# Token preparation by rows: most token tiles modulated and split token-major, then turned by transposing transfers

## Chip, cores and metric

The kernel runs on one core of one Trainium2 chip. The metric is the device time of one launch in microseconds (us), the median of the runs shown. Engines are named as the profile names them: PE is TensorE (its weight loads are PEld), DVE is VectorE, ACT is ScalarE, POOL is GpSimd, SP is SyncE, which here only issues transfers.

## What is computed

Two layers over 2048 latent and 256 context tokens of width 1024. Each layer is an RMS norm with a modulation (a scale and a shift per feature, one pair for the latent stream and one for the context), an input projection, four token mixers with SiLU gates (Fourier, attention, convolution, pooling), and an output projection:

```
h  = rmsnorm(x,  norm_g) * (1.0 + scale)   + shift       # latent, 2048 x 1024
hc = rmsnorm(xc, norm_g) * (1.0 + scale_c) + shift_c     # context, 256 x 1024
parts = split(h @ w_in)                                  # q, k, v, Fourier u, gates, conv, pool inputs
out   = concat([o_f, o_att, o_c, o_p]) @ w_out
x_new = x + gate * out                                   # and the same for xc in layer 0
```

The change is in how the kernel builds `h` and `hc` in the form that the input projection wants.

## The kernel before, in words

The tokens lie in five blocks: b0 is the 256 context tokens, b1 to b4 are 512 latent tokens each. A block is prepared in tiles of 128 tokens, four to a latent block and two to the context, 36 over both layers. `prep(L, b)` turns a block into tiles `h{b}{part}{i}`: features on the partitions, tokens along the row, as a pair of 16-bit numbers (part 0 the rounded value, part 1 the remainder), since the products on PE are made of three 16-bit passes.

For one tile of 128 tokens `prep` loads it (L251), squares and sums it on ACT (L261), makes the reciprocal root on POOL (L240, L241), scales the tile by it on ACT (L263), turns it on PE by eight 128x128 transposes into PSUM (L271), applies scale and shift on DVE, which reads that PSUM (L275, eight instructions, one for each 128 features), rounds to 16 bits on ACT (L278) and takes the remainder on POOL (L279). It is a generator and yields once for each tile, so that its caller can lay the tiles between other work.

The token stage of a layer is `token_groups`. Its `block(b)` makes the products that are wanted token by token: two `fourier_in` (48 matmuls of 256 columns each, L342), `keys` and `values` (96 of 128 columns each, L332), and two `queries` (L342 again). `keys` and `queries` go on through norm and rotary positions: POOL does L240, L241, L407 (the rotary table times the gain), L438, L451 and L461, and DVE does L420, L431, L436 and L440. Their results are stored by SP: `kd` (L452), `qd` (L462), and the Fourier input `ud` (L376). Each yield of `block(b)` runs one step of the preparation of a later block: in layer 0 of the next one, in layer 1 of the one two places on, in the order b1, b2, b3, b4, b0. Layer 1 prepares b1 and b2 beside the end of layer 0's output projection (L1166). PE then goes from the last queries of one block straight to the first `fourier_in` of the next, which reads all features of the tokens it covers.

A scheduler decides the final order of the instructions; each engine then runs its own list in that order and waits by semaphores. Tiles come from pools with a fixed number of buffers; a tile is reused when its last reader is done. `dg` (L1120, L1125) is an existing helper of the output projection: a diagonal matrix is multiplied by a matrix of ones on PE, so that a row of 512 numbers stands on all partitions.

Of the kernel before, what the change touches and what calls it, by code (L numbers as in the profile page):

```python
# [10 lines left out]
F32 = mybir.dt.float32  # L11
F32R = mybir.dt.float32r
F16 = mybir.dt.float16
BF16 = mybir.dt.bfloat16
ACTF = mybir.ActivationFunctionType
ALU = mybir.AluOpType
# [4 lines left out]
D = 1024  # L21
KC = 8
# [4 lines left out]
BLK = [(0, 256)] + [(256 + 512 * i, 512) for i in range(4)]  # L27
# [15 lines left out]
def hybrid_kernel(ctx: ExitStack, tc: tile.TileContext, T, out):  # L43
    nc = tc.nc
    PE, ACT, DVE, POOL, SP = nc.tensor, nc.scalar, nc.vector, nc.gpsimd, nc.sync
# [18 lines left out]
    sm = pool("sm", 3)  # L64
# [16 lines left out]
    def big(shape, dt, name):  # L81
        return slot.tile(shape, dt, tag="s", name=name)
# [13 lines left out]
    id32 = const.tile([128, 128], F32, name="id32")  # L96
# [10 lines left out]
    ones = const.tile([128, 128], F32, name="ones")  # L107
# [96 lines left out]
    aff = {}  # L204
# [23 lines left out]
    def alloc_h(b):  # L228
        n = BLK[b][1]
        per = 2048 // n  # L230
        hT[b] = [[big([128, per, n], F16, f"h{b}{part}{i}") for i in range(KC // per)] for part in range(2)]

    def h_ap(b, part, k, t0, n, nk=1):
        per = 2048 // BLK[b][1]
        t = hT[b][part][k // per]
        return t[:, k % per, t0:t0 + n] if nk == 1 else t[:, k % per:k % per + nk, t0:t0 + n]

    def rms_scale(ss, n, count, tag):
        ms = sm.tile([128, 8], F32, tag=tag, name=tag)[:, 0:n]
        POOL.tensor_scalar(out=ms, in0=ss, scalar1=1.0 / count, scalar2=EPS, op0=ALU.mult, op1=ALU.add)  # L240
        POOL.tensor_tensor(out=ms, in0=ms, in1=nh[:, 0:n], op=ALU.pow)  # L241
        return ms

    def prep(L, b, tp, psum):

        s = 1 if b == 0 else 0
        g0, n = BLK[b]

        def load(t):
            xt = tp.tile([128, D], F32, tag="x", name="xt")  # L250
            (SP if L == 0 and b < 2 else ACT).dma_start(out=xt, in_=source(L, g0 + t * 128))  # L251
            return xt

        ahead = load(0)
        for t in range(n // 128):
            xt = ahead
            if (t + 1) * 128 < n:
                ahead = load(t + 1)
            xn = tp.tile([128, D], F32, tag="xn", name="xn")
            ss = sm.tile([128, 1], F32, tag="ss", name="ss")  # L260
            ACT.activation(out=xn, in_=xt, func=ACTF.Square, accum_out=ss)  # L261
            rstd = rms_scale(ss, 1, D, "rx")
            ACT.activation(out=xn, in_=xt, func=ACTF.Copy, scale=rstd)  # L263
            yield
            if t == 0:
                alloc_h(b)
            for half in range(2):
                pt = psum()
                for j in range(4):
                    k = 4 * half + j  # L270
                    PE.transpose(out=pt[:, j * 128:(j + 1) * 128], in_=xn[:, k * 128:(k + 1) * 128], identity=id32)  # L271
                h32 = tp.tile([128, 4, 128], F32, tag="h32", name="h32")
                for j in range(4):
                    k = 4 * half + j
                    DVE.tensor_scalar(out=h32[:, j, :], in0=pt[:, j * 128:(j + 1) * 128], scalar1=aff[L][0][:, 0, k, s:s + 1],  # L275
                                      scalar2=aff[L][0][:, 1, k, s:s + 1], op0=ALU.mult, op1=ALU.add)
                hi = h_ap(b, 0, 4 * half, t * 128, 128, 4)
                ACT.copy(out=hi, in_=h32)  # L278
                POOL.tensor_tensor(out=h_ap(b, 1, 4 * half, t * 128, 128, 4), in0=h32, in1=hi, op=ALU.subtract)  # L279
# [849 lines left out]
    def source(L, tok):  # L1129

        if L > 0:
            return xd[tok:tok + 128]
        return T["ctx"][tok:tok + 128] if tok < NCTX else T["x"][tok - NCTX:tok - NCTX + 128]
# [51 lines left out]
    TOKEN = {"s": 4, "ko": 1, "qo": 1, "rope": 1, "gq": 1}  # L1185

    gate_w = {}
    with ExitStack() as st:
        tp = TagPool(st, tc, "s0", {**TOKEN, "x": 4, "xn": 2, "h32": 2, "row": 1})
        ws = []  # L1190
        ahead = prep(0, 0, tp, aux_bank)
        for c in range(4):
            for i, _ in enumerate(modulate(0, c, aux_bank, tp, True)):
                if (c, i) == (0, 3):
                    steps(ahead, 1)
                if (c, i) == (2, 3):
                    ws += [load_w(0, *TOKEN_W[0])]
        SP.dma_start(out=gain, in_=T["gains"].partition_broadcast(128))
        ws += [load_w(0, *TOKEN_W[1])]
        SP.dma_start(out=edge, in_=T["k_edge"])  # L1200
        SP.dma_start(out=invw, in_=T["k_invw"])
        SP.dma_start(out=cd, in_=T["k_cd"])
        affine(0)
        for w in ws:
            unscale(0, w[1])
        steps(ahead, 9)
        block = token_groups(0, tp, ws)
        for b in range(5):
            ahead = prep(0, b + 1, tp, aux_bank) if b + 1 < 5 else iter(())
            if b == 4:  # L1210
                gate_w[0] = load_w(0, *GATE_W[0:2], True)
            for _ in block(b):
                steps(ahead, 1)
            steps(ahead, 9)
# [27 lines left out]
    for L in range(DEPTH):  # L1242
# [19 lines left out]
        right = ExitStack()  # L1262
# [19 lines left out]
        with ExitStack() as st:  # L1282
            pp = TagPool(st, tc, f"p{L}", {"mix": 1, "ml": 2, "gate": 1, "x": 2})
            late = project(L, blocks[-2:], lambda shape, dt, name: pp.tile(shape, dt, "mix" if name == "dg" else name, name), 2)
            steps(late, 1)
            steps(fill, 1 << 30)
            if L + 1 < DEPTH:
                w_mode(f"t{L + 1}", True)
                with ExitStack() as st2:
                    sp = TagPool(st2, tc, f"s{L + 1}", {**TOKEN, "s": 2, "x": 2, "xn": 1, "h32": 2}, "right")  # L1290
                    with tc.issue_after(load_mark[0]):
                        block = token_groups(L + 1, sp, [])
                    for b in blocks[0:2]:
                        for _ in prep(L + 1, b, sp, mx_bank):
                            steps(late, 3)
                    for i, b in enumerate(blocks):
                        ahead = prep(L + 1, blocks[i + 2], sp, mx_bank) if i + 2 < 5 else iter(())
                        if i == 3:
                            gate_w[L + 1] = load_w(L + 1, *GATE_W[0:2], True)
                        for _ in block(b):  # L1300
                            steps(ahead, 1)
                            steps(late, 8)
                        steps(ahead, 9)
                        if i == 0:
                            steps(late, 1 << 30)
            steps(late, 1 << 30)
# [98 lines left out]
```

## Time and profile before

| what | value |
|---|---|
| time, median of 3 runs | 2219.25 us (2217.25 to 2222.85) |
| the profiled execution's own time | 2221.17 us |
| its span, first to last instruction | 2219.4 us |
| granted clock of PE, mean | 0.990 |
| busy, share of the span | PE 96%, DVE 64%, ACT 55%, POOL 42% |
| layer 0's token stage, blocks b1 to b4 | 67.7 to 205.2 us |
| layer 1's token stage with the end of the projection | about 1094 to 1330 us |

The profile is one execution. Its page gives the busy time of each engine and a strip of 40 slices of the span; its views give groups of instructions by line, a timeline, and sums over windows. A granted clock of 1.00 is the full speed of PE (2.4 GHz), 0.50 the lower level (1.2 GHz). "What ended an idle time" is the instruction whose semaphore came last.

### The profile page before, as it was taken

What the parts mean: (1) busy time and instruction counts of PE and PEld (TensorE: products, weight loads), DVE (VectorE), ACT (ScalarE), POOL (GpSimd) and SP (SyncE); (2) the same over time, 40 slices, a digit from 0 to 9 for tenths busy, and PEclk for the clock granted to TensorE, in tenths of its full rate; (3) what the DMA queues carried; (4) which work ended last, traced back from release to release, by engine and by line L of the source; (5) the groups of instructions that cost most, each with busy time, mean ns of one, the idle gap of its engine ahead of it and who ended that gap; (6) DMA issues with size and microseconds to landing.
All of it is one profiled execution on the core that took longest, in us unless ns stands there. A gap on an engine that the chain in (4) does not pass through costs nothing. (4 is left out here: it accounts for less than half of the span.)

```text
span 2219.4 us, 41113 instructions
## 1 busy us (share of the span) xinstructions
PE 2136.6 (96%) x16207; PEld 1287.1 (58%) x16207; DVE 1411.0 (64%) x2661; ACT 1216.8 (55%) x2265; POOL 931.7 (42%) x998
## 2 busy tenths in 40 slices
PE   7999989989999999999899999999999999989999
PEld 3998545655556555555456995555455555555544
DVE  3654777456687878676575554522678787877533
ACT  4653445346677767555554534334477676766600
POOL 2786543214455556233233862001356355543300
PEclk9999989999999999999999999999999999999999
DMA  8433554551212122222454333335221221223133
GB/s 324 141 101 96 178 165 160 203 155 48 65 46 69 58 71 79 95 71 69 171 200 134 118 100 114 110 105 169 71 65 33 68 63 46 72 88 99 42 102 123
DMA packets 182639, 237.95 MB, mean 107 GB/s; under 512 B 47178, under 2 KB 132526, under 8 KB 182446
## 3 DMA queue, kind: packets, MB, share of 16 engines
q1 hardware_dynamic: 159854, 205.96, 28.4%
q10 hardware_dynamic: 22592, 29.37, 4.2%
q8 instruction: 127, 2.08, 0.4%
q14 instruction: 66, 0.54, 0.1%
HBM read 161.48 MB, written 69.34 MB: 104 GB/s over the span
## 5 line engine op out<-in xcount | busy, mean ns | idle before, releaser
L319 PE MATMUL fl<-h,w 128*128 128x512 f16 (+1 forms) x2592 | 595.5, 368 | 0.4 <-ACT z L504 0.2
L1007 POOL TENSOR_TENSOR pl<-p,ph 128x512 f16<-128x512 f32 (+1 forms) x292 | 355.2, 1216 | 517.9 <-ACT p L1006 435.0
L319 PEld LDWEIGHTS <-w 128*128 128x128 f16 x3456 | 331.2, 99 | 362.0 <-issue 38.8
L1005 ACT ACTIVATE ph<-st 128x512 f16<-128x512 f32 (+1 forms) x584 | 348.7, 597 | 239.2 <-PE st L1001 213.3
L959 DVE TENSOR_REDUCE mp<-mx 128x1 f32<-128x512 f32 (+1 forms) x648 | 394.7, 627 | 114.4 <-PE mx L958 111.7
L1166 PE MATMUL fl<-wo,ml 128*128 128x512 f16 x1632 | 378.9, 380 | 1.4 <-ACT gate L1126 1.1
L1006 ACT ACTIVATE p<-st 128x512 f32<-128x512 f32 (+1 forms) x584 | 349.0, 598 | 25.2 <-DVE pl L1007 23.7
L1007 DVE TENSOR_TENSOR pl<-p,ph 128x512 f16<-128x512 f32 (+1 forms) x292 | 233.1, 798 | 83.5 <-ACT p L1006 67.9
L1166 PEld LDWEIGHTS <-ml 128*128 128x128 f16 x1632 | 158.9, 98 | 184.2 <-issue 6.4
L995 PEld LDWEIGHTS <-ph 128*128 128x128 f16 x2320 | 169.6, 98 | 124.3 <-ACT ph L1005 26.8
L995 PE MATMUL pv<-V,ph 128*128 128x130 f16 x2320 | 222.7, 220 | 11.3 <-ACT ph L1005 10.9
L958 PE MATMUL mx<-kst,qhh 128*128 128x512 f16 x512 | 188.1, 379 | 15.2 <-DVE mp L959 12.2
L319 PE MATMUL st<-h,w 128*128 128x512 f16 (+1 forms) x864 | 195.4, 376 | 3.6 <-DVE r L436 3.6
L1000 PE MATMUL st<-qhh,kst 128*128 128x512 f16 x512 | 193.9, 379 | 2.5 <-ACT p L1006 2.3
L1001 PE MATMUL st<-qlm,k 65*128 65x512 f16 x512 | 195.1, 381 | 0.0
L993 PE MATMUL pv<-V,pl 128*128 128x66 f16 x2320 | 169.1, 193 | 4.1 <-DVE pl L1007 2.1
L342 PEld LDWEIGHTS <-h 128*128 128x128 f16 x1632 | 159.9, 98 | 20.6 <-POOL h L279 0.7
L993 PEld LDWEIGHTS <-pl 128*128 128x128 f16 x2320 | 132.6, 97 | 44.0 <-POOL pl L1007 6.0
L1171 DVE TENSOR_TENSOR fl<-fl,gate 128x512 f32<-128x512 f32 x68 | 47.4, 697 | 99.8 <-PE fl L1166 99.7
L145 POOL TENSOR_TENSOR root<-root,ph__105 128x2 f32<-128x2 f32 (+1 forms) x28 | 20.3, 726 | 207.6 <-DVE root L144 197.7
L157 ACT ACTIVATE ml<-mix,f 128x1024 f16<-128x1024 f32 x34 | 39.1, 1151 | 113.6 <-PE fl L1166 80.3
L332 PEld LDWEIGHTS <-h 128*128 128x128 f16 x1728 | 98.5, 98 | 0.7
(300 smaller groups left out, 3024.4 us busy)
## 6 DMA issues: line engine op xcount, KB each, us to landing
wm<-in_w_mod_dram SPq DMA_DIRECT2D x48, 512.0 KB, 4.5
wst<-in_w_in_dram SPq DMA_DIRECT2D x44, 512.0 KB, 4.2
mix<-mixd SPq DMA_DIRECT2D x34, 512.0 KB, 4.4
zd<-z SPq DMA_DIRECT2D x64, 256.0 KB, 2.2
wst<-in_w_out_dram SPq DMA_DIRECT2D x32, 512.0 KB, 4.5
xd<-x SPq DMA_DIRECT2D x18, 512.0 KB, 3.0
xt<-xd ACTq DMA_DIRECT2D x18, 512.0 KB, 4.4
x<-in_x_dram SPq DMA_DIRECT2D x16, 512.0 KB, 5.2
```

The lines of the kernel that those rows point to most:

```text
L319: last = PE.matmul(out=ps, lhsT=w[:, wp, k, :], rhs=h_ap(b, hp, k, 0, n), start=(k == 0 and i == 0), stop=(k == KC - 1 and i == 2))
L342: PE.matmul(out=ps[:, t], lhsT=h_ap(b, hp, k, (2 * i + t) * 128, 128), rhs=w[:, :, wp, k, :], start=(k == 0 and j == 0), stop=(k == KC - 1 ...
L958: mark[0] = PE.matmul(out=ps, lhsT=qhh[:, t * 128:(t + 1) * 128], rhs=kk, start=True, stop=True).ins
L959: DVE.tensor_reduce(out=mp[:, t, i:i + 1], in_=ps, axis=AX.X, op=ALU.max)
L993: PE.matmul(out=pv[t // 2][:, t % 2, 0:66], lhsT=p, rhs=v[:, 0:66], start=False, stop=(kt == nk - 1), skip_group_check=True)
L995: PE.matmul(out=pv[t // 2][:, t % 2, :], lhsT=p, rhs=v, start=(kt == 0 and t % 2 == 0), stop=False, skip_group_check=True)
L1000: mark[0] = PE.matmul(out=ps, lhsT=self.k_tile(0, kt), rhs=qhh, start=True, stop=False).ins
L1001: PE.matmul(out=ps, lhsT=self.k_tile(1, kt)[0:65, :], rhs=qlm[0:65, :], start=False, stop=True)
L1005: ACT.activation(out=ph, in_=ps, func=ACTF.Exp, scale=1.0 / LOGIT)
L1006: ACT.activation(out=p32, in_=ps, func=ACTF.Exp, scale=1.0 / LOGIT)
L1007: (POOL if kt % 2 == 0 else DVE).tensor_tensor(out=pl, in0=p32, in1=ph, op=ALU.subtract)
L1166: PE.matmul(out=ps, lhsT=ml[:, mp, k, :], rhs=wo[k][:, wp, half * 512:(half + 1) * 512], start=(k == 0 and j == 0), stop=(k == KC - 1 and ...
```

## The change

For layer 1, and for b2, b3 and b4 of layer 0, `prep` hands over to a new function, `prep_rows`; the two tiles of b0 and the four of b1 in layer 0 stay as they were. That is 30 of the 36 tiles. A tile stays token-major through norm, modulation and split; DVE multiplies it by the reciprocal root and the scale row (L290) and adds the shift row (L291); ACT rounds it (L292); POOL takes the remainder (L293); and SP turns the two halves by transposing transfers from SBUF to SBUF (L276). A latent tile needs four of these, a context tile two, 116 in all. They are issued when the next tile has been worked on. The scale and shift rows are made once for each layer and stream (three times) by `affine_rows`: two diagonal tiles on DVE (L250), four matmuls with ones (L255), four copies on ACT.

```
-            (SP if L == 0 and b < 2 else ACT).dma_start(out=xt, in_=source(L, g0 + t * 128))
+            SP.dma_start(out=xt, in_=source(L, g0 + t * 128))      # in prep, now only layer 0, b0 and b1
+        if L or b > 1:
+            yield from prep_rows(L, b, tp, psum)
+            return
...
+    def affine_rows(L, s, psum):
+        for a in range(2):
+            dg = big([128, 8, 128], F32, "dg")
+            DVE.tensor_tensor(out=dg, in0=id32.unsqueeze(1).to_broadcast([128, 8, 128]),
+                              in1=aff[L][0][:, a, :, s].unsqueeze(2).to_broadcast([128, 8, 128]), op=ALU.mult)
+            r = big([128, 1024], F32, f"row{a}")
+            for half in range(2):
+                pg = psum()
+                PE.matmul(out=pg, lhsT=ones, rhs=dg[:, 4 * half:4 * half + 4, :].rearrange("p j f -> p (j f)"), start=True, stop=True)
+                ACT.copy(out=r[:, half * 512:(half + 1) * 512], in_=pg)
+            rows[L, s, a] = r
...
+        def turn(t, hl):
+            for part in range(2):
+                for i in range(KC // per):
+                    SP.dma_start_transpose(out=h_ap(b, part, per * i, t * 128, 128, per), in_=hl[:, part, per * 128 * i:per * 128 * (i + 1)])
+        ahead, past = load(0), None
+        for t in range(n // 128):
...
+            hl = tp.tile([128, 2, D], F16, tag="hl", name="hl")
+            ss = sm.tile([128, 1], F32, tag="ss", name="ss")
+            ACT.activation(out=hl.rearrange("p a f -> p (a f)").bitcast(F32), in_=xt, func=ACTF.Square, accum_out=ss)
+            rstd = rms_scale(ss, 1, D, "rx")
+            yield
+            if t == 0:
+                alloc_h(b)
+            DVE.scalar_tensor_tensor(out=xt, in0=xt, scalar=rstd, in1=rows[L, s, 0], op0=ALU.mult, op1=ALU.mult)
+            DVE.tensor_tensor(out=xt, in0=xt, in1=rows[L, s, 1], op=ALU.add)
+            ACT.copy(out=hl[:, 0], in_=xt)
+            POOL.tensor_tensor(out=hl[:, 1], in0=xt, in1=hl[:, 0], op=ALU.subtract)
+            if past:
+                turn(*past)
+            past = t, hl
+        yield
+        turn(*past)
...
-        tp = TagPool(st, tc, "s0", {**TOKEN, "x": 4, "xn": 2, "h32": 2, "row": 1})
+        tp = TagPool(st, tc, "s0", {**TOKEN, "x": 4, "xn": 2, "h32": 2, "hl": 2, "row": 1})
-                    sp = TagPool(st2, tc, f"s{L + 1}", {**TOKEN, "s": 2, "x": 2, "xn": 1, "h32": 2}, "right")
+                    sp = TagPool(st2, tc, f"s{L + 1}", {**TOKEN, "s": 2, "x": 2, "hl": 2}, "right")
```

Outside layer 0's token stage and the passage from layer 0 to layer 1 with layer 1's token stage, every engine has its instructions in the same order as before. Lines behind the new functions stand 59 lower in the changed kernel: L342 is L401, L440 is L499, L452 is L511.

Transfers issued by SP, layer 0, while block b2's products run, where `kd` is the store of that block's keys. Before:

```order
L462 DMA qd_92<-qo_1396 128x2x768
L376 DMA ud_95<-u_1550 128x2x256
L405 DMA rope_1839<-in_k_rope_dram 128x2x256
L452 DMA kd_93<-ko_1703 128x4x256
L405 DMA rope_2161<-in_k_rope_dram 128x2x256
L462 DMA qd_92<-qo_1933 128x2x768
```

And in the changed kernel around the same store, where `hl` is a token tile in its two halves and `h3` the turned block b3:

```order
L276 DMA_TRANSPOSE h311_1419<-hl_1426 128x4x128
L464 DMA rope_1736<-in_k_rope_dram 128x2x256
L276 DMA_TRANSPOSE h300_1416<-hl_1499 128x4x128
L511 DMA kd_93<-ko_1617 128x4x256
L276 DMA_TRANSPOSE h301_1417<-hl_1499 128x4x128
L276 DMA_TRANSPOSE h310_1418<-hl_1499 128x4x128
L276 DMA_TRANSPOSE h311_1419<-hl_1499 128x4x128
L276 DMA_TRANSPOSE h300_1416<-hl_1629 128x4x128
L276 DMA_TRANSPOSE h301_1417<-hl_1629 128x4x128
L276 DMA_TRANSPOSE h310_1418<-hl_1629 128x4x128
L276 DMA_TRANSPOSE h311_1419<-hl_1629 128x4x128
L464 DMA rope_2024<-in_k_rope_dram 128x2x256
```

Of the sixteen transposes of b3, seven stand behind the key store of b2: three of the third tile's and all of the last one's.

DVE in layer 0, beside block b2's products. Before, the preparation of b3 reads PSUM (`fl`, `mx`):

```order
L275 TENSOR_SCALAR h32_1473<-fl_1468,ab_304 128x128 x4
L275 TENSOR_SCALAR h32_1485<-mx_1480,ab_304 128x128 x4
L440 TENSOR_TENSOR q_1389<-q_1389,rq_1384 128x512
L275 TENSOR_SCALAR h32_1563<-fl_1558,ab_304 128x128 x4
L275 TENSOR_SCALAR h32_1575<-mx_1570,ab_304 128x128 x4
```

In the changed kernel it reads SBUF alone (`xt` is the token tile, `row0` and `row1` the scale and shift rows):

```order
L499 TENSOR_TENSOR q_1268<-q_1268,rq_1263 128x512
L290 SCALAR_TENSOR_TENSOR xt_1353<-xt_1353,rx_1360,row0_798 128x1024
L291 TENSOR_TENSOR xt_1353<-xt_1353,row1_807 128x1024
L499 TENSOR_TENSOR q_1342<-q_1342,rq_1337 128x512
L290 SCALAR_TENSOR_TENSOR xt_1355<-xt_1355,rx_1429,row0_798 128x1024
L291 TENSOR_TENSOR xt_1355<-xt_1355,row1_807 128x1024
```

Eight instructions of 128x128 a tile have become two of 128x1024.

PE in layer 1, inside block b3's first `fourier_in`. Before, the turning of a context tile stands behind the product, 271 being the transposes:

```order
L342 LDWEIGHTS h311_15452
L342 MATMUL pv_16739<-w_14802,h311_15452 128x256
L271 MATMUL mx_16794<-id32_97,xn_16732 128x128 x4
L271 MATMUL mx_16806<-id32_97,xn_16732 128x128 x4
L342 LDWEIGHTS h300_15449
L342 MATMUL st_16825<-w_14802,h300_15449 128x256
```

In the changed kernel the matmuls that make the context's shift row stand inside the product:

```order
L401 LDWEIGHTS h311_15207
L401 MATMUL pv_16317<-w_14617,h311_15207 128x256
L255 MATMUL mx_16301<-dg_16298,ones_107 128x512
L401 LDWEIGHTS h300_15204
L401 MATMUL pv_16317<-w_14617,h300_15204 128x256
L255 MATMUL mx_16304<-dg_16298,ones_107 128x512
L401 LDWEIGHTS h300_15204
```

The transposes are gone from PE's list, and two matmuls that read `dg` from DVE have come into the middle of a product. On DVE that `dg` stands behind the two pairs of the last latent block and a block's rotary work:

```order
L291 TENSOR_TENSOR xt_15821<-xt_15821,row1_14694 128x1024
L290 SCALAR_TENSOR_TENSOR xt_15894<-xt_15894,rx_16029,row0_14685 128x1024
L291 TENSOR_TENSOR xt_15894<-xt_15894,row1_14694 128x1024
L479 TENSOR_REDUCE ssq_16001<-sq_15999 128x8
L490 TENSOR_TENSOR q_16007<-pv_15902,rope_15882 128x512
L495 TENSOR_TENSOR r_16009<-pv_15902,rope_15882 128x8x32 x2
L499 TENSOR_TENSOR q_16007<-q_16007,rq_16003 128x512
L442 TENSOR_REDUCE vms_14604<-vr_16129 128x1
L479 TENSOR_REDUCE ssq_16197<-sq_16194 128x8
L490 TENSOR_TENSOR q_16204<-pv_16145,rope_16133 128x512
L495 TENSOR_TENSOR r_16206<-pv_16145,rope_16133 128x8x32 x2
L250 TENSOR_TENSOR dg_16298<-id32_97,ab_5252 128x1024
```

The first row ends one pair, the two behind it are another; in the kernel before neither the pairs nor `dg` stood there.

## Rows read from the trace of the kernel before

**Rows 1.** The page: busy time by engine.

```profile
PE 2136.6 (96%) x16207; PEld 1287.1 (58%) x16207; DVE 1411.0 (64%) x2661; ACT 1216.8 (55%) x2265; POOL 931.7 (42%) x998
```

**Rows 2.** Windows of layer 0: blocks b1, b2 and b4.

```profile
core 0: us, PE busy (x) PEld busy (x) DVE busy (x) ACT busy (x) POOL busy (x), PEclk, DMA share, GB/s
67.70:103.00 35.30, 35.30 (x420) 33.16 (x418) 20.90 (x54) 24.32 (x40) 29.23 (x38) 1.00 0.42 134
103.00:138.18 35.18, 35.18 (x418) 32.99 (x416) 19.97 (x49) 20.66 (x33) 29.97 (x38) 1.00 0.33 108
...
173.51:205.20 31.69, 31.69 (x388) 29.50 (x387) 13.37 (x22) 9.37 (x15) 19.63 (x23) 1.00 0.34 110
```

**Rows 3.** Windows of layer 1's token stage, same columns.

```profile
1134.10:1206.88 72.78, 72.09 (x413) 41.50 (x412) 43.85 (x97) 37.44 (x55) 29.28 (x36) 1.00 0.50 166
...
1229.84:1265.03 35.19, 35.19 (x418) 33.00 (x416) 18.85 (x48) 20.46 (x33) 29.09 (x38) 1.00 0.42 129
1265.03:1298.00 32.97, 32.97 (x398) 30.85 (x396) 13.80 (x32) 13.65 (x24) 22.62 (x28) 1.00 0.23 73
```

**Rows 4.** Timeline of PE, layer 1: a tile's eight transposes (start, us, ...).

```profile
1276.61 1.04 PE L271 MATMUL mx<-id,xn 128*128 128x128 f32 x8
1277.49 1.73 PE L332 MATMUL pv<-w,h 128*128 128x128 f16 x28
```

**Rows 5.** Timeline of PE: two matmuls with ones, two records each.

```profile
1175.67 1.88 PE L1125 MATMUL fl<-dg,ones 128*128 128x512 f32 x4
1177.39 1.36 PE L342 MATMUL st<-w,h 128*128 128x256 f16 x11
```

**Rows 6.** Lines of DVE, whole span: ns minimum/median/maximum of one.

```profile
L275 DVE TENSOR_SCALAR h<-mx,ab x216: 393/402/412, 42.2 to 1280.8; 128x128 f32<-128x128 f32 x108
...
L158 DVE SCALAR_TENSOR_TENSOR w<-wst,ws,w x44: 1268/1282/2294, 31.9 to 1694.9; 128x1024 f16<-128x1024 f32 x44
...
L1120 DVE TENSOR_TENSOR dg<-id,modT x5: 1206/1209/1687, 776.0 to 1964.4; 128x1024 f32<-128x1024 f32 x5
...
L440 DVE TENSOR_TENSOR q<-q,rq x27: 426/693/1622, 67.3 to 1349.6; 128x512 f32<-128x512 f32 x25, 128x256 f32<-128x256 f32 x2
```

**Rows 7.** Timeline of POOL and DVE, layer 0's Fourier stage.

```profile
231.56 2.08 POOL L728 TENSOR_TENSOR u<-u,u 128x896 f32<-128x896 f32 x1 [2.12 <-DVE oo L728]
231.60 2.46 DVE L728 TENSOR_TENSOR cd__3282<-oo 128x384 f32<-128x384 f32 x1
```

**Rows 8.** Groups of POOL in 103.00 to 138.18: count, busy us, mean ns.

```profile
L241 POOL TENSOR_TENSOR rq<-rq,nh 128x8 f32<-128x8 f32 x4 | 6.6, 1650 | 0.2
L438 POOL TENSOR_TENSOR q<-q,r 128x512 f32<-128x512 f32 x3 | 3.8, 1271 | 0.0
L407 POOL TENSOR_TENSOR rope<-rope,gq 128x256 f32<-128x256 f32 x4 | 3.7, 952 | 0.0
```

**Rows 9.** The line of POOL L407 over the whole span.

```profile
L407 POOL TENSOR_TENSOR rope<-rope,gq x32: 723/730/2049, 42.8 to 1329.8; 128x256 f32<-128x256 f32 x32
```

**Rows 10.** SP's transposing transfers of attention, 128 KB each, out of DRAM.

```profile
L949 SPq DMA_TRANSPOSE qhh<-qd x36: 1103/1130/2297, 441.8 to 2009.0; - x36
...
DMA to landing us min/median/max: 2.3/2.6/6.9
```

**Rows 11.** Timeline of PE and SP: block b2's keys product, and the keys' store.

```profile
115.22 5.52 PE L332 MATMUL pv<-w,h 128*128 128x128 f16 x96
...
135.05 0.36 SPq L452 DMA_DIRECT2D kd<-ko  x1
```

**Rows 12.** Windows after a wait of PE in layer 0's projection (columns as rows 2).

```profile
1095.00:1097.00 2.00, 2.00 (x6) 0.64 (x5) 0.73 (x3) 0.67 (x2) 0.41 (x1) 0.50 0.71 204
1097.00:1099.00 2.00, 2.00 (x9) 0.86 (x8) 0.00 (x0) 0.77 (x1) 0.00 (x0) 0.79 1.08 422
```

**Rows 13.** Timeline of PE there: the wait in brackets.

```profile
1094.88 1.87 PE L1166 MATMUL fl<-wo,ml 128*128 128x512 f16 x4 [1.10 <-ACT gate L1126]
```

More of the change, by code (lines that the diff above doesn't have):

```diff
@@ L242, in rms_scale @@
         return ms
+    rows = {}
+    def affine_rows(L, s, psum):
[9 more added lines that the diff above has]
+            rows[L, s, a] = r
@@ new lines, in prep_rows, with load @@
+    def prep_rows(L, b, tp, psum):
+        g0, n = BLK[b]
+        s = 1 if b == 0 else 0
+        per = 2048 // n
+        if (L, s, 0) not in rows:
+            affine_rows(L, s, psum)
+        def load(t):
+            xt = tp.tile([128, D], F32, tag="x", name="xt")
+            ACT.dma_start(out=xt, in_=source(L, g0 + t * 128))
+            return xt
+        def turn(t, hl):
[4 more added lines that the diff above has]
+        for t in range(n // 128):
+            xt = ahead
+            if (t + 1) * 128 < n:
+                ahead = load(t + 1)
+            hl = tp.tile([128, 2, D], F16, tag="hl", name="hl")
[14 more added lines that the diff above has]
+        turn(*past)
```

## Prediction

> **What bounds the kernel now.** I read the page first: PE is busy 96% of the span, POOL 42%, DVE 64% [rows 1]. An average says little of the stages that the change touches, so I cut the token stage into windows from one block's first product to the next one's. There PE's busy time equals the window, at full clock: 35.30 and 35.18 us for blocks that carry a preparation, 31.69 for b4, which carries none [rows 2]. PE sets the pace, and the 3.5 us between the two are the preparation's transposes. The second engine is POOL: 29.97 of 35.18 us, 85%, double its mean over the span. Layer 1 is looser: beside the projection POOL has 29.28 of 72.78 us, and only the block at 1229.84 has the picture of layer 0 (29.09 of 35.19) [rows 3]. So the change removes work from the engine that bounds, and what has to be asked is how near the others come.
>
> **PE.** A tile's eight transposes begin at 1276.61 and the next product at 1277.49: 0.88 us [rows 4]. 30 tiles give 26.4 us. Added are twelve matmuls with ones; two of the same size took 1177.39 − 1175.67 = 1.72 us, 0.86 each [rows 5], so 10.3 in all: 3.4 in layer 0, 6.9 in layer 1. Net −16.1 us, if nothing else becomes late.
>
> **DVE and POOL.** DVE's old affine step cost eight times 0.40 us a tile and read PSUM; its duration stays between 393 and 412 ns over 216 instructions, whatever POOL does beside it [rows 6]. The new step is two instructions of 128x1024 with both inputs in SBUF. The nearest rows are L158 (1.28, same operation, but 16-bit output) and L1120 (1.21) [rows 6]: 2.5 us a tile at their medians, 3.97 at their maxima (2.29 + 1.69). DVE has room for that: 19.97 of 35.18 us is busy, and 3.2 of each tile goes away [rows 2].
>
> But the two kinds of instruction differ beside POOL. In layer 0's Fourier stage POOL and DVE begin instructions with SBUF inputs 0.04 us apart: POOL's takes 2.08 us, and DVE's, of only 384 elements, 2.46 [rows 7], while a DVE instruction of 1024 elements takes 1.28 alone. It waited for POOL's whole instruction. L440, also from SBUF alone, goes from 0.69 to 1.62 [rows 6], and POOL's L407 is stretched the other way, 0.95 on average in block b2 against a median of 0.73 [rows 8, 9]. So I treat POOL and those DVE instructions as users of one lane, one at a time.
>
> The Trainium skill states this as a rule (page "SBUF — State Buffer", section "Who interferes with whom"): a VectorE instruction with two SBUF inputs and a GpSimd instruction that reads SBUF lock each other out for the whole instruction. By that rule the change moves DVE's work from where it never meets POOL to where it always does; the rows above agree.
>
> The lane in block b2's window: POOL 29.97, less 4 × 0.22 that L407 already waits [rows 8, 9], gives 29.1; L440 three times 0.69 is 2.1; four tiles at 2.5 are 10.0. Sum 41.2 us. PE would need 35.18 − 4 × 0.88 = 31.7. The lane is therefore the bound, 6.0 over the old window. POOL's own work does not fall, since four subtractions of 1024 replace eight of 512. Three windows of layer 0 (b1 to b3) carry four changed tiles, and one of layer 1 (1229.84): 4 × 6.0 = **+24 us**. b3's window in layer 1 holds two context tiles: 22.62 + 2.1 + 5.0 = 29.7 of 32.97 [rows 3], no bound. Bounds per loaded window: 31.7 − 35.2 = −3.5 where nothing collides, and 29.1 + 2.1 + 4 × 3.97 − 35.2 = +11.9 at the maxima.
>
> PE's gain then counts only elsewhere: 14 tiles of layer 1 (18 less the four of the loaded window), 14 × 0.88 = 12.3, less 6.9 for layer 1's ones-matmuls: **−5.4 us**. Layer 0's 3.4 lie in a window where PE waits.
>
> **Waits of PE and its clock.** Where the lane is late, PE stands at a block's first `fourier_in` until the turned tiles have landed. In the projection, after a wait of 1.10 us [rows 13], the granted clock was 0.50 (the 1.2 GHz level) for 2 us and 0.79 for the next two [rows 12]: 1.0 + 0.4 = 1.4 us lost. Four such waits: **+6 us** (0 if the waits are short, 10 if each loaded window has two).
>
> **Transposing transfers.** No row has one out of SBUF. Nearest are attention's, out of DRAM: 1.13 us of SP's time to issue, 2.30 at most, 2.6 us to land, 6.9 at most [rows 10]. A plain store takes 0.36 [rows 11], the lower bound. At 1.13 a block's sixteen take 18.1 of some 40 us of SP, which issues little else here. The place matters more: seven of them stand behind b2's keys store, and SP works in order. That store went out at 135.05, 3.1 us before b3's first product at 138.18, though the keys' product had ended at 120.7 [rows 2, 11]. Seven issues and a landing are 7 × 1.13 + 2.6 = 10.5 us. If the store stays where it is, b3's tiles land 7.4 us late; if it goes as soon as the norm's POOL steps allow (120.7 + 1.65 + 1.27 at the least [rows 8]), they are ready 4 us early. The delay runs beside the lane's and ends in the same wait, so I add nothing here; 7.4 − 6.0 = 1.4 a window is the price if the store does not move.
>
> The Trainium skill (page "Advanced Engine Details and Errata", section "X-Bar Transpose (TRN2)") says that transposing transfers are as fast as regular ones. By that sentence sixteen issues would cost SP 5.8 us, not 18.1; the issue rows here disagree, threefold, and the row decides.
>
> **Context rows in layer 1.** Two ones-matmuls stand in the middle of a product of b3 and read `dg`, which DVE builds behind two pairs and a block's rotary work. PE takes its list in order, so all products behind wait. Two pairs are 5.0 us and `dg` 1.2; in the lane each may double. I take two waits of 5, one for each `dg`: **+10 us**; 0 if DVE is ahead, 12 if both wait for two pairs and a `dg`. For the latent rows and the first tiles of layer 1, issued beside the projection, **+2** (0 to 4).
>
> ACT keeps its square, trades a scaling and two casts of 0.6 for one cast of 1024, and has room (20.66 of 35.18) [rows 2]: nothing.
>
> **Sum.** 24 − 5.4 + 6 + 10 + 2 = +36.6 us. The profiled execution took 2221.17 against the median of 2219.25, so 2257.8 on its own scale, and 2256 on the median's, which I give.
>
> **Rivals.**
> - *The lane is no bound (the other side).* POOL's instructions and DVE's would interleave without loss; PE's 16.1 us show. At seven block starts the last transposes come some 1.3 us late (between 4 early and 7.4 late): −16 + 9 = −7, 2212 us. For it: POOL alone fits, 30 of 31.7 us. Against it: rows 7. It decides where a window's lane sum is under 31.7.
> - *Slack between windows takes the lateness up.* b4's window has 31.7 − 19.6 = 12 us of POOL free; POOL's rotary work can slip there, so only 18 − 12 = 6 of layer 0's 18 stay, and layer 1's 6 go into b3's window. 6 − 5.4 + 10 + 2 + 3 of clock = +16, 2235 us. Against it: the subtractions themselves cannot slip past the block that reads them.
> - *Transfers out of SBUF cost more to issue.* At 1.9 us, between the median and the maximum: 7 × 1.9 + 2.6 − 3.1 = 12.8 late at each of four starts, 51 instead of 24, so +64 and 2283 us. At 2.3 sixteen take 36.8 us of SP, and it becomes the bound: about 2300.
> - *The change does not do what it says:* the transposes are gone from PE's list, so no.
>
> **How the numbers follow.** Lane as computed, 2256: 0.55 (own range 2240 to 2270). Slack, 2235: 0.13. Dearer transfers, 2283 to 2300 and beyond: 0.18. Lane no bound, 2212: 0.14, of which half is within 0.3% (6.7 us, about what a measurement of this kernel can tell from no change) and half is faster by more. A little of the slack case is also within 0.3%. So faster 0.08, same 0.10, slower 0.82. The range leaves out most of the last rival and the far end of the dear transfers: 2218 to 2305.
>
> **What would show it.** Right: PE waits at the first products of b2, b3 and b4, released by the transposing transfers; windows of 40 us and more for 35.2; clock below 1.00 behind those waits; the two new DVE lines well over their 1.28 and 1.21; POOL's lines stretched; PE waiting for `dg` in b3's first product of layer 1. Wrong: windows of about 32 us with PE at full busy time and unstretched DVE lines (no lane), or DVE and POOL idle while SP's issues follow each other at 2 us (the transfers bound).

## Result and the profile after

The changed kernel takes 2277.57 us (median of 4, 2270.87 to 2278.80) against 2219.98 for the kernel before on the same chip: a ratio of 1.0257, interval 1.0238 to 1.0275, **57 us slower**. Forecast were 2256 us, with 2240 to 2270 if the lane came as computed, and a range of 2218 to 2305 over all cases. The profiled execution has a span of 2276.9 us at a mean clock of 0.977. Its page, as [rows 1]:

```profile
PE 2140.3 (94%) x15991; PEld 1271.9 (56%) x15991; DVE 1441.0 (63%) x2487; ACT 1185.7 (52%) x2217; POOL 945.8 (42%) x968
```

No engine's total tells the loss; the stages do. I cut both spans at the first gate product of layer 0 (205.2 us before, 231.3 after), at layer 0's last attention product (1093.6, 1125.8) and at the first gate product of layer 1 (1335.6, 1389.0). Layer 0 up to the end of its token stage lost 26.1 us, layer 1's passage and token stage 21.2, the stretch between 6.1 and the rest 4.1: together the 57.5 by which the spans differ.

Layer 0's windows for b1 to b4, as [rows 2]:

```profile
69.30:104.42 35.12, 35.12 (x395) 30.68 (x392) 18.25 (x28) 14.32 (x25) 21.79 (x22) 1.00 0.54 107
104.42:147.38 42.96, 33.46 (x386) 29.78 (x384) 22.57 (x23) 13.60 (x23) 31.51 (x31) 0.92 0.72 144
147.38:190.66 43.28, 34.20 (x388) 30.08 (x386) 25.66 (x25) 18.58 (x31) 34.67 (x33) 0.88 0.60 133
190.66:231.32 40.66, 36.01 (x387) 30.97 (x386) 23.77 (x32) 12.74 (x21) 32.73 (x35) 0.87 0.49 140
```

The lateness shows one window after the one that causes it: b1's 35 us are kept, b2 to b4 take 43.0, 43.3 and 40.7 instead of 35.2, 35.3 and 31.7. PE waits in them (columns: us in total, times, longest) in one place alone:

```profile
PE st L401 <- DMA h<-hl: 23.2, 10, 7.9
```

That is the second `fourier_in` of a block, the one that wants the third and fourth tile. PE's timeline of b3 shows where:

```profile
147.38 5.40 PE L401 MATMUL pv<-w,h 128*128 128x256 f16 x48
153.29 0.39 PE L401 MATMUL st<-w,h 128*128 128x256 f16 x2 [0.51 <-DMA h<-hl]
161.55 2.74 PE L401 MATMUL st<-w,h 128*128 128x256 f16 x12 [7.86 <-DMA h<-hl]
```

The transfers are late because their tiles are. POOL and DVE in b3's preparation, beside b2's products, from the timeline:

```profile
125.22 1.65 POOL L241 TENSOR_TENSOR rq<-rq,nh 128x8 f32<-128x8 f32 x1
...
127.44 2.17 DVE L290 SCALAR_TENSOR_TENSOR xt<-xt,rx,row 128x1024 f32<-128x1024 f32 x1 [9.11 <-POOL rx L241]
...
128.51 2.49 POOL L486 TENSOR_SCALAR rq<-rq,winv 128x4 f32<-128x4 f32 x2
...
133.58 2.13 POOL L293 TENSOR_TENSOR hl<-xt,hl 128x1024 f16<-128x1024 f32 x1
133.65 3.15 DVE L290 SCALAR_TENSOR_TENSOR xt<-xt,rx,row 128x1024 f32<-128x1024 f32 x1 [1.41 <-POOL rx L241]
...
135.67 2.14 POOL L520 TENSOR_TENSOR qo<-q,qo 128x512 f16<-128x512 f32 x1
136.83 2.06 DVE L291 TENSOR_TENSOR xt<-xt,row 128x1024 f32<-128x1024 f32 x1
```

DVE's 1.28 us instruction takes 3.15 where it begins behind POOL's subtraction, POOL's 1.16 us subtraction 2.14 where DVE was first, and two scalings of 0.27 take 2.49. That is the lane, in both directions: each is held until about the end of the other's instruction (POOL's subtraction ends at 135.71, DVE's instruction at 136.80). But another wait stands beside it that the prediction has not: ACT's square of the third tile writes into an `hl` buffer, and there are two of them. The lines of L276 (SP's issues), over the whole span, say who waited for a landing:

```profile
L276 SPq DMA_TRANSPOSE h<-hl x116: 1188/1257/2680, 85.1 to 1333.8; - x116
...
  ACT hl L285: 70.6, 20
  PEld L401: 27.1, 11
  PE st L401: 23.2, 10
...
DMA to landing us min/median/max: 2.4/3.9/8.5
```

In layer 0's stage ACT's square stood for a landing at five of twelve tiles, 16.7 us in all. One issue costs 1.26 us (1.13 assumed [rows 10]); in a row they cost more, eight at 109.62 take 12.29 us. A pair of tiles goes through square, POOL, DVE, ACT, POOL, eight issues and a landing before its two buffers are free: some 21.5 us, 43 for four tiles. That figure is read off the pace itself, so it does not decide. Two theories give the windows seen: the **lane** (41 us a block, the prediction's) and the **ring** (the round of the two `hl` buffers). The expectations below name a third, the **issue** theory: SP's sixteen issues a block, seven of them behind the keys' store, set the pace. b3's start shows what speaks for it:

```profile
153.91 0.39 SPq L511 DMA_DIRECT2D kd<-ko  x1
154.36 10.36 SPq L276 DMA_TRANSPOSE h<-hl  x7
...
157.31 2.12 POOL L293 TENSOR_TENSOR hl<-xt,hl 128x1024 f16<-128x1024 f32 x1
...
166.91 2.58 PE L401 MATMUL st<-w,h 128*128 128x256 f16 x22 [0.38 <-DMA h<-hl]
```

The last tile's subtraction ends at 159.43; its transposes are issued until 164.72, and PE goes on at 166.91.

In layer 1 the ring shows where POOL is mostly free. Window 1136 to 1224, beside the projection, has 25.25 us of POOL in 88:

```profile
1136.00:1224.00 88.00, 78.92 (x378) 38.15 (x377) 54.46 (x64) 31.29 (x41) 25.25 (x23) 0.98 0.81 193
```

PE works 78.92 us there, idle for 9.1, and 87.31 in the like stretch of the kernel before, idle for 0.7:

```profile
1105.00:1193.00 88.00, 87.31 (x476) 47.74 (x475) 57.93 (x122) 46.20 (x64) 30.61 (x38) 1.00 0.54 179
```

Followed back from one of its waits in the timeline:

```profile
1168.91 5.86 SPq L276 DMA_TRANSPOSE h<-hl  x4
...
1180.03 1.06 ACT L285 ACTIVATE hl<-xt 128x1024 f32<-128x1024 f32 x1 [9.16 <-DMA h<-hl]
...
1182.13 1.29 DVE L290 SCALAR_TENSOR_TENSOR xt<-xt,rx,row 128x1024 f32<-128x1024 f32 x1 [7.41 <-POOL rx L241]
...
1185.32 0.69 DVE L1231 TENSOR_TENSOR x<-x,fl 128x512 f32<-128x512 f32 x1
...
1186.06 5.34 PE L1225 MATMUL fl<-wo,ml 128*128 128x512 f16 x24 [1.67 <-DVE x L1231]
```

A transfer holds the buffer, ACT waits, so POOL, so DVE; and behind DVE's waiting L290 stands L1231 of the projection, which has nothing to do with the tile, and for which PE waits. PE's waits of layer 1's stage:

```profile
PE mx L255 <- ACT row L256: 9.8, 1, 9.8
PE fl L1225 <- DVE x L1231: 6.8, 4, 3.7
PE st L391 <- DVE r L495: 3.7, 1, 3.7
PE fl L1184 <- ACT gate L1185: 2.3, 1, 2.3
PE fl L1225 <- ACT ml L157: 1.9, 1, 1.9
```

### The profile page after: what moved, and what is told of

Same layout as the page of the kernel before. It is cut to its first block, busy times and chain, and to the rows that moved or that the text cites. A ratio compares the mean times of both kernels' runs of the same rounds, so it can differ in the third digit from the quotient of the medians.

```text
span 2276.9 us, 40619 instructions
## 1 busy us (share of the span) xinstructions
PE 2140.3 (94%) x15991; PEld 1271.9 (56%) x15991; DVE 1441.0 (63%) x2487; ACT 1185.7 (52%) x2217; POOL 945.8 (42%) x968
## 5 line engine op out<-in xcount | busy, mean ns | idle before, releaser
L401 PEld LDWEIGHTS <-h 128*128 128x128 f16 x1632 | 162.1, 100 | 56.2 <-DMA h<-hl 27.1
L401 PE MATMUL st<-w,h 128*128 128x256 f16 x816 | 100.7, 284 | 23.2 <-DMA h<-hl 23.2
L145 POOL TENSOR_TENSOR root<-root,ph__105 128x2 f32<-128x2 f32 (+1 forms) x28 | 19.9, 711 | 206.5 <-DVE root L144 197.6
L391 PEld LDWEIGHTS <-h 128*128 128x128 f16 x1728 | 100.9, 100 | 5.2 <-issue 3.9
```

The costliest lines, as they stand in the source:

```text
L401: PE.matmul(out=ps[:, t], lhsT=h_ap(b, hp, k, (2 * i + t) * 128, 128), rhs=w[:, :, wp, k, :], start=(k == 0 and j == 0), stop=(k == KC - 1 ...
```

## Experiments

All start from the changed kernel; ratios are to the kernel before, run beside them. "L0" is the end of layer 0's token stage, "L1" the length of layer 1's, both from the profiled execution.

| run | ratio (95%) | L0, us | L1, us |
|---|---|---|---|
| before | 1 | 205.2 | 242.1 |
| after | 1.0257 (1.0238 to 1.0275) | 231.3 | 263.3 |
| once | 1.0227 (1.0206 to 1.0249) | 225.4 | 261.9 |
| half | 1.0199 (1.0179 to 1.0218) | 214.1 | 254.8 |
| lean | 1.0178 (1.0157 to 1.0198) | 223.7 | 265.0 |
| junk | 1.0171 (1.0146 to 1.0196) | 219.1 | 260.8 |
| junkonce | 1.0180 (1.0153 to 1.0207) | 216.9 | 264.6 |
| all3 | 1.0224 (1.0200 to 1.0247) | 221.1 | 254.8 |
| jos | 1.0144 (1.0116 to 1.0171) | 210.5 | 252.3 |
| jos4 | 1.0113 (1.0083 to 1.0143) | 211.2 | 255.6 |
| nolane | 1.0190 (1.0170 to 1.0211) | 206.5 | 272.0 |
| jo4n | 1.0151 (1.0125 to 1.0177) | 209.4 | 256.2 |
| ctxrows | 1.0233 (1.0205 to 1.0261) | 228.8 | 259.2 |
| l0only | 1.0148 (1.0131 to 1.0166) | 230.1 | 240.5 |

**once**: transposes right behind their tile.

```
-            if past:
-                turn(*past)
-            past = t, hl
-        yield
-        turn(*past)
+            turn(t, hl)
```

> The transposes of a tile are issued right behind its remainder instead of one tile later; nothing else differs. Ring theory (two hl buffers, each free again only when its turned tile has landed; a pair of tiles takes about 21.5 us, so a block of four 43): a buffer's round is then about 16 us, two buffers give a tile every 8 us, a block needs 32, and PE hardly waits in layer 0: about 2250 us (2240 to 2260). Lane theory (POOL and VectorE's SBUF instructions share one lane, 41 us a block): the lane's sum does not change, 2277 within 5. Issue theory (SP's 16 issues of about 1.5 us a block, seven behind the keys' store): 16 issues stay, the order hardly changes, 2270 to 2280.

2274 us: 6 us of layer 0's 26. The ring theory had PE hardly wait and the whole at 2250, so the lag by one tile is not what makes a round long, or the ring alone is not the limit.

**half**: `if part == 0:` before the transposing transfer, and both parts of `hT[b]` the same tiles.

> Only the rounded halves are turned: 58 transposing transfers instead of 116; the third pass of the products reads the rounded half again, so the remainder's part of h is left out where the tokens are prepared by rows. All engines' other instructions stay. Ring theory: a pair's round loses four to eight issues of 1.5 us (21.5 to about 14), a block needs 28 to 31, PE no longer waits in layer 0: about 2245 us (2235 to 2255). Issue theory: the same, 2235 to 2255. Lane theory: the lane's 41 us a block stay, only the last tile's issues are shorter: 2265 to 2277.

Layer 0's stage ended at 214.1, 17 us earlier, and PE waits only 2.0 us for turned tiles there, which speaks for ring and issue theory; but b2 and b3 took 36.6 and 40.3 us, not the 28 to 31 that the ring theory had. The whole, 2268.5, is in the lane's range: it fell by 13 only (by the ratios). The stretch from layer 0's gates to its last attention product took 907 us here (894 in the changed kernel, 888 before), which no theory had. all3, with the same alias of the two parts, shows 907 there too; how the alias does it is not settled.

**lean**: `ACT.activation(..., func=ACTF.Copy, scale=0.0)` for POOL's remainder in `keys` and `queries`.

> The remainders of queries and keys (three or four instructions of 1.16 us a block on POOL) are left out: ACT writes zeros there instead. POOL, and with it the shared lane, loses 3.5 to 4.6 us a block, outside the path of a token tile. Lane theory: four loaded windows times 3.5 to 4.6, 2259 to 2263 us. Ring theory: the path of a tile does not run through these, 2270 to 2277. Issue theory: the keys' store may go out 1 us earlier, 2272 to 2277.

2263.0 us, inside the lane's range and outside the others'. POOL work off the tiles' path costs time, as the lane has it. But only 7.6 of layer 0's 26 us came back and none in layer 1 (265.0); the rest of the fall lies outside the two stages, so that the total fits is partly luck.

**junk**: the square's unused output.

```
-            ACT.activation(out=hl.rearrange("p a f -> p (a f)").bitcast(F32), in_=xt, func=ACTF.Square, accum_out=ss)
+            ACT.activation(out=tp.tile([128, D], BF16, tag="jk", name="jk"), in_=xt, func=ACTF.Square, accum_out=ss)
```

> ACT's square writes its unused result into a small 16-bit tile of its own instead of into the hl buffer (layer 0's pool of token tiles goes from four buffers to three to make room); the hl buffer is then wanted only when the modulated tile is rounded. Ring theory: square, reciprocal root and the two VectorE instructions (1.2 + 0.8 + 2.5 us and their queues) leave the buffer's round; 21.5 a pair goes to about 17, a block to 34: 2250 us (2242 to 2262). Lane theory: 2277 within 5. Issue theory: 2270 to 2280.

2261.0 us, inside the ring's range: the early claim on the buffer costs 12 us in layer 0. After four runs the whole times of once, half and lean lay in the lane's ranges and that of junk in the ring's.

**junkonce**: junk and once.

> The square into a tile of its own and the transposes right behind the tile, nothing else (all 116 transfers, the remainder on POOL). Ring theory: the two alone gave 13.9 and 20.2 us over the kernel before in layer 0's token stage, against 26.1 with neither; together about 8 (stage end 213), the whole 2250 to 2256. Lane theory: no earlier than 220 us, 2262 or more. Issue theory: 2262 or more, since sixteen issues a block stay.

Stage end 216.9, between the two; the whole 2264 (no gain over junk within the intervals), which is in the lane's and the issue theory's range and not in the ring's.

**all3**: junk, once and half together, so that no ring should hold.

> Three edits at once: only the rounded halves are turned (58 transfers; the remainder's part of h is left out where tokens are prepared by rows), they are issued right behind the tile, and the square writes into a tile of its own. POOL's and VectorE's instructions all stay, so the lane theory's 41 us a loaded block stay too. Lane theory: layer 0's token stage ends no earlier than 205 + 15 = 220 us, the whole 2255 or more. Ring theory (the round of the two hl buffers, through square, POOL, VectorE, ACT, POOL, SP's issues and the landing, sets the pace): the round falls under what PE needs, layer 0's stage ends by about 200 to 206 us, the whole 2225 to 2242.

PE no longer waits for a turned tile in layer 0, but the stage ends at 221.1, on the lane's side. Its windows of b2 and b3 and PE's waits there:

```profile
104.16:147.69 43.53, 33.39 (x387) 30.76 (x385) 27.13 (x25) 19.61 (x32) 38.45 (x36) 0.95 0.51 144
147.69:189.40 41.71, 35.73 (x386) 32.67 (x387) 25.30 (x29) 15.80 (x27) 36.22 (x38) 0.89 0.41 114
```

```profile
PE pv L388 <- DVE r L492: 11.3, 2, 6.0
PE pv L398 <- DVE r L492: 4.9, 1, 4.9
```

POOL is busy 38.45 and 36.22 us, and the wait has moved: PE now stands for a PSUM bank that DVE's rotary work empties late. With the ring relaxed the lane is nearly full: added up from the traces, POOL or one of the DVE instructions with SBUF inputs alone (L290, L291, L499 and their like) is at work 79.7 of these 85.2 us, 93%, against 107.6 of 126.9 us, 85%, in b2 to b4 of the changed kernel. But the 42 to 43 us a block are not the lane's sum alone: half, with the same work in the lane, has 36.6 and 40.3 us for these blocks. There more of that work slipped into b4's window (29.3 us of it, 24.0 here).

**jos**: junk, once, and the remainder on DVE (`DVE.tensor_tensor(out=hl[:, 1], ...)`), which takes POOL's 2.13 us a tile down to some 1.2 in the lane.

> The square into a tile of its own, the transposes right behind the tile, and the remainder taken by VectorE (1.2 us) instead of POOL (2.13). Lane theory: the lane's sum falls by 4 x (2.13 - 1.2) = 3.7 us a loaded block, 41.2 to 37.5: 2277 - 15 = 2262. Ring theory: POOL's queue (which a tile passes twice, and before once) gets 8.5 us a block shorter and the path 0.9 us: layer 0's stage ends at 206 to 212 us, the whole 2238 to 2250. Issue theory (SP's sixteen issues of 1.5 us a block, seven behind the keys' store): 2255 or more.

Stage end 210.5, inside the ring theory's range; the whole is 2254.7, above that theory's 2238 to 2250, under the lane's 2262 and just at the issue theory's 2255. b2 and b3 take 40.5 and 34.1 us; their mean, 37.3, lies at the lane's sum of 37.5, but neither block does, so this is no test of the sum. All work is done in it.

**jos4**: as jos, with the square into layer 0's `xn` tile, so that four token tiles stay.

> All work in place: square into another tile with four token tiles kept, transposes right behind the tile, the remainder on VectorE (1.2 us) instead of POOL (2.13). Both-limits theory: lane 37.5 us a loaded block instead of 41, the round relaxed, token tiles loaded earlier than in the run with three of them: layer 0's stage ends at 205 to 210 us (210.5 there), the whole 2243 to 2254. Lane theory alone 2262; issue theory 2255 or more. None of them forecasts a time under that of the kernel before.

2248.4 us, inside the forecast of both limits; the stage end, 211.2, is 1.2 past it and as in jos. That jos and its relatives have three token tiles cost nothing in layer 0.

**nolane**: the pair replaced by two reductions of like length that read one SBUF tile each, and two tiny instructions.

```
-            DVE.scalar_tensor_tensor(out=xt, in0=xt, scalar=rstd, in1=rows[L, s, 0], op0=ALU.mult, op1=ALU.mult)
-            DVE.tensor_tensor(out=xt, in0=xt, in1=rows[L, s, 1], op=ALU.add)
-            ACT.copy(out=hl[:, 0], in_=xt)
+            m = sm.tile([128, 2], F32, tag="mm", name="mm")
+            DVE.tensor_scalar(out=m[:, 1:2], in0=rstd, scalar1=1.0, scalar2=None, op0=ALU.mult)
+            DVE.tensor_reduce(out=m[:, 0:1], in_=xt, axis=AX.X, op=ALU.max, apply_absolute_value=True)
+            DVE.tensor_reduce(out=m[:, 0:1], in_=xt, axis=AX.X, op=ALU.max, apply_absolute_value=True)
+            DVE.tensor_tensor(out=m[:, 1:2], in0=m[:, 0:1], in1=m[:, 1:2], op=ALU.mult)
+            ACT.activation(out=hl[:, 0], in_=xt, func=ACTF.Copy, scale=m[:, 1:2])
```

> The two VectorE instructions of a tile are replaced by two reductions over the same 128x1024 tile with one input each (1.2 to 1.3 us each, and two tiny ones), and ACT rounds with a factor from them: the path of a tile and every queue stay as long, but VectorE no longer needs POOL's lane; the modulation is left out. Lane theory alone: the lane's sum falls to 31 us a loaded block, layer 0's token stage ends by 205, the whole 2245 or less. Ring theory alone (round of the two hl buffers): 2272 to 2280. Both limits close together, as the earlier runs suggest: what the pairs waited in the lane leaves the round (14 us over layer 0's twelve tiles), but the round itself stays: stage end 220 to 226, the whole 2258 to 2270.

Layer 0's stage ends at 206.5: 25 of its 26 us are back, with all 116 transfers, the two buffers and the lag as they were. Windows of b2, b3, b4:

```profile
107.58:139.26 31.68, 31.68 (x386) 29.51 (x384) 20.71 (x31) 13.02 (x20) 24.19 (x29) 1.00 0.79 183
139.26:173.81 34.55, 32.46 (x388) 29.61 (x386) 17.71 (x30) 17.52 (x29) 26.12 (x31) 1.00 0.72 138
173.81:206.53 32.72, 32.00 (x384) 29.32 (x385) 15.37 (x26) 11.09 (x19) 25.02 (x30) 1.00 0.61 164
```

POOL's lines of b2's window are short again:

```profile
L523 POOL TENSOR_TENSOR qo<-q,qo 128x512 f16<-128x512 f32 x2 | 2.3, 1159 | 0.8 <-ACT qo L522 0.8
...
L513 POOL TENSOR_TENSOR ko<-q,ko 128x512 f16<-128x512 f32 x1 | 1.2, 1153 | 0.1
L489 POOL TENSOR_SCALAR rq<-rq,winv 128x4 f32<-128x4 f32 x4 | 1.0, 270 | 0.0
```

against the same three in the changed kernel's b2:

```profile
L520 POOL TENSOR_TENSOR qo<-q,qo 128x512 f16<-128x512 f32 x2 | 3.3, 1649 | 0.0
L486 POOL TENSOR_SCALAR rq<-rq,winv 128x4 f32<-128x4 f32 x4 | 3.0, 765 | 0.0
...
L510 POOL TENSOR_TENSOR ko<-q,ko 128x512 f16<-128x512 f32 x1 | 2.1, 2135 | 0.0
```

The edit is not pure. The tiles no longer need the modulation rows, and the scheduler begins b2's preparation earlier. And the path of a tile did not stay as long as the expectation says: the reductions need no reciprocal root and run ahead of it. DVE's order shows it (L291 copies the root, L294 makes the factor that ACT waits for):

```profile
128.62 0.15 DVE L291 TENSOR_SCALAR mm<-rx 128x1 f32<-128x1 f32 x1 [1.95 <-POOL rx L241]
128.69 1.21 DVE L292 TENSOR_REDUCE mm<-xt 128x1 f32<-128x1024 f32 x1
129.82 0.77 DVE L294 TENSOR_TENSOR mm<-mm 128x1 f32<-128x1 f32 x1
130.51 1.21 DVE L293 TENSOR_REDUCE mm<-xt 128x1 f32<-128x1024 f32 x1
```

The factor needs both reductions of its tile, so the two seen here belong to the next tile: one stands on the path, not two. From L291's start to L294's end it is 1.35 us where nothing collides, against 2.55 for the pair; over layer 0's tiles the means are 2.3 and 5.0. So the 25 us are the lane, a path shorter by 1.2 us a tile and the earlier start. The ring with that path would by estimate still need some 38 us a block (21.4 − 2.4 a pair, twice), not the 31.7 to 34.6 seen, so the lane's part is the larger; its exact size is open. Layer 1 did not gain (272.0): the whole is 2262.9, so the lane's forecast of the total (2245) failed there; that of both limits (2258 to 2270) holds it, but missed the stage end (220 to 226) by 14. With sixteen issues a block as before, the stage's end also shows that the issues alone are not the limit.

**jo4n**: nolane with the ring relaxed too.

> As the last (reductions in place of the pair, the modulation left out), and also both edits that relax the hl buffers' round: the square into another tile (in layer 0 the free tile of the first blocks, so that the pool of token tiles keeps its four), the transposes right behind the tile. Both-limits theory: neither limit is left, PE sets layer 0's pace, stage end 196 to 205 us, the whole 2235 to 2250 with layer 1's waits. Lane theory alone: the same as without the two edits. Ring theory alone: the same as the two edits with the pair in place, stage end about 213. If the issue of sixteen transposes a block (1.5 us each) is a third limit: stage end 210 or later.

Stage end 209.4, not better than nolane (206.5) and past the forecast 196 to 205; the whole, 2255.4, is past 2235 to 2250 too. The issue theory's 210 is near, but PE waits only 1.3 us for turned tiles in that stage. Layer 1's 256.2 is better by 16 than nolane's. So in layer 0 nothing is left to gain from the ring once the lane is free; layer 1 answers to the ring where the pair is gone, though with the pair (junkonce, 264.6) it did not.

**ctxrows**: `s = 0` in `prep_rows`.

> Layer 1's context block takes the latent stream's scale and shift rows, so the context's own (two diagonal tiles on VectorE, four ones-matmuls, four copies) are left out in layer 1. The trace of the changed kernel shows one wait of 9.8 us of PE there, at a ones-matmul that waits for ACT's copies of the rows before it. If that wait is a loss of its own, the time falls by 9.8 + 1.7 (two of the four matmuls' pairs) + 1.4 of clock: 2264 to 2268. If PE would have waited there anyhow (for the block's products' readers), 2272 to 2277.

The 9.8 us wait is gone, but the whole falls by 2.6 us by the medians and 5 by the ratios, with overlapping intervals: other waits (`DVE r L495`, 3.7 and 0.4 in the changed kernel, here 7.6 and 3.4) took its place. PE's waits in layer 1's stage are 25.9 us in all in the changed kernel and 21.9 here. By these two traces the wait was mostly where lateness came to light, not its cause.

**l0only**: `if L == 0 and b > 1`.

> Layer 1 prepares its tokens as in the kernel before; layer 0's b2, b3 and b4 by rows. Layer 1's stage took 242.1 us before and 263.3 after, layer 0's 205.2 and 231.3. If the two layers' losses add: 2220 + 26 to 32, 2246 to 2252 us. If layer 1's loss came from layer 0's order or from something else that the change moved, the time stays nearer 2277.

2254.5 us, 2 us over what was forecast, and layer 1's stage is back at 240.5. The losses add: about 33 us for layer 0's part and 24 for layer 1's. No kernel here beats the one before.

## Why the prediction was right, point by point

The direction and the mechanism came as forecast; the size did not, +57.5 us in the traces for +36.6. The time, 2277.6 us, lies above the lane's own range (2240 to 2270) and nearer to the 2283 of the dearer transfers, which did not come. That the wide range holds it is owed to that rival and is luck in part. Of the 20.9 us too little, layer 0 has 3.6 (26.1 for 22.5), layer 1 has 7.1 and the two stretches for which nothing was forecast 10.2.

- *PE sets the pace, and its 26 us come off its list.* Right: 16207 matmul records became 15991, and blocks without waits take 31.7 us (nolane's b2).
- *The lane, 41.2 us a loaded block.* Right in mechanism; the pair came out at 1.28 and 1.23 us alone, 3.15 and 3.04 at most. Three windows took 43.0, 43.3 and 40.7, +24.7 us with their waits and lowered clock, against 18 + 4.5 forecast for layer 0. That this is so close is partly luck (next point). The stretched instructions on both engines, lean and nolane show that the lane costs time; nolane's 25 us contain a shorter path as well. A sum of before's numbers fits: POOL's 108.8 us in the four windows [rows 2, and b3's 29.96], less 12 × 0.22, plus twelve times L440 and twelve pairs (8.3 + 30) is 144.5, so by this estimate layer 0's stage should not end before 67.7 + 144.5 = 212 us. No kernel with pair and POOL subtraction did (214.1 was the earliest, by half); those that lower the floor reached 206 to 211. It is no sharp limit: half's b1 began at 70.4, so its stage took 143.7 us.
- *What the step lacked:* that the lane is reached through a ring. The change's `hl` has two buffers, the square claims one at a tile's start, and the transfers give it back last. The pool was in the diff, and I priced no wait for it. The lane by itself, with b4's free time used, asks for 212 − 205 = 7 us and not 18, as the rival on slack had it (6). The changed kernel stands 19 us over that floor, with the lane at work 85% of b2 to b4, and half and junk, which leave the lane's sum alone and shorten the ring, gave back 17 and 12 of them.
- *PE waits at a block's first `fourier_in`.* The place was off: the first has its two tiles, the second waits (23.2 us in ten waits, not four). The clock fell as said, to 0.87 to 0.92 over the windows, but cost more: PE's busy time there is 103.7 us for 3 × 31.7, 8.6 more, where 4.5 was forecast for layer 0.
- *Transposing issues 1.13 us.* Measured 1.26, in rows up to 1.5; the rival of dearer transfers (1.9) did not come. The keys' store did not go out earlier but later: at 107.46, 153.91 and 198.44, which is 3.0, 6.5 and 7.8 us behind the next block's first product, where it had been 1.6, 3.1 and 5.2 ahead. And the issues, to which the forecast gave nothing because they run beside the lane, run partly behind it: from the end of a block's last subtraction to PE's last start in the product that waits it is 8.2, 7.5 and 2.9 us.
- *Context rows +10.* A wait of 9.8 came, at ACT's copies rather than at `dg`; the run without it gave back 2.6 to 5 us, not clear of noise. The term seems too large by half or more.
- *First tiles of layer 1, +2 (0 to 4).* Mis-sized: beside the projection PE stood idle 9.1 us of 88, where it had been 0.7. The trace shows one such wait from transfer to PE, through engines that work in order. Layer 1 as a whole lost 21.2 us where its terms (6 + 1.5 − 5.4 + 10 + 2) gave 14. How the 21 divide is not settled: fewer transfers (half) gave back 8.5, the remainder on DVE (jos against junkonce) 12, while relaxing the ring alone (junk, junkonce) gave 2.5 and nothing.
- *Nothing outside the two stages.* The traces show +6.1 and +4.1 us there, though the order is the same. The first stretch took 891 to 907 us in all thirteen traces with rows and 888 in the one trace before, so it may belong to the change; the second scatters from 884 to 895. With one trace of the kernel before, whether that is the change or the execution stays open.

## What to carry to other kernels

Before moving work from PE and PSUM to SBUF, add up for each stage POOL's time and the VectorE instructions whose inputs all lie in SBUF: they shared one lane here, and no kernel with both kinds of work had a stage much shorter than the sum (143.7 us the shortest, for a sum of 144.5). A tile whose last user is a transfer makes a ring: the length of its whole round, times tiles over buffers, was a second limit here; claim the buffer as late as the data allows. And a wait on an engine that works in order is paid by whatever stands behind it, here by a projection that shared nothing with the late tile.

## What the runs showed of the hardware

- Transposing transfers out of SBUF cost SP 1.26 us each to issue at the median (1.13 out of DRAM); back to back 1.3 to 1.5 (eight in 12.29). 116 of them raised the packets under 512 bytes from 47178 to 112330.
- A reduction of 128x1024 with one SBUF input held 1202 to 1222 ns over 30 instructions beside a busy POOL, where the pair went from 1.28 to 3.15. But a product of two 128x1 numbers in SBUF, 0.16 us alone, took up to 2.12: the lane is a matter of the operands, not of the size.

```profile
L292 DVE TENSOR_REDUCE mm<-xt x30: 1202/1213/1222, 54.4 to 1276.3; 128x1 f32<-128x1024 f32 x30
...
L294 DVE TENSOR_TENSOR mm<-mm x30: 148/160/2122, 68.7 to 1283.1; 128x1 f32<-128x1 f32 x30
```
